# A two-layer encoder trunk on one core: output products of a feed-forward group issued behind the sixth product of the next group, and fewer accumulating transfers at a layer's middle

## The chip, the cores and the metric

The kernel runs on one core of a Trainium2 chip. The metric is the device time of one execution in microseconds; lower is better. Five engines of the core work side by side, each in the order of its own instruction stream: TensorE (PE in the profile; its weight loads are PEld), VectorE (DVE), ScalarE (ACT), GpSimd (POOL) and SyncE (SP). Sixteen DMA engines move data; in this kernel SP issues plain transfers and POOL the accumulating ones, which add what they read to what stands in on-chip memory.

## The reference

Two layers. Each normalises its input, projects it, mixes tokens by windowed pooling and by differential attention, adds the gated sum back, and then adds a gated feed-forward block:

```python
for i in range(DEPTH):                                  # 2 layers, x is 512 x 1024, float32
    proj = rmsnorm(x, norm1_g[i]) @ w_in[i]             # u_pool, q, k, v, g_a, g_b
    ...
    o = diff_attention(q, k, v, lam)
    attn_out = (rmsnorm(o, subln_g[i]) * (1.0 - lam_init)) ...
    pool_out = pool_mixer(u_pool, pool_w[i], pool_scale[i])
    merged = sigmoid(g_a) * pool_out + sigmoid(g_b) * attn_out
    x = x + merged @ w_out[i]
    gate, up = split(rmsnorm(x, norm2_g[i]) @ w_ffn_in[i], 2)   # hidden width 2816
    x = x + (silu(gate) * up) @ w_ffn_out[i]
return x
```

## The kernel before

**Number format.** Every product of two float32 matrices is three TensorE products: each operand is held as a high part (a rounded copy) and a low part (the difference), and high x high, high x low and low x high are summed (L280 to L282 and L299 to L301). A weight piece of 512 KB is loaded to a tile `raw` (L224, by SP, 7 buffers) and split into `whi` and `wlo` (6 buffers each). There are two ways to make the low part in `parts`: ACT copies the high part and DVE subtracts (L210, L211), or ACT writes the high part and the negated raw piece (L234, L235) and an accumulating transfer issued by POOL adds the raw piece from HBM once more (L236).

**A layer.** Four heads of attention and pooling run first; `last_out` then adds the second half of the `w_out` product to the residual `res`, 4 pieces of 2 products, and after each piece `Sets.put` makes operands of the new `res` for the feed-forward block. The feed-forward block has 22 hidden tiles of 128. The two odd ones (`odd_group`, tiles 20 and 21) are computed plainly. The other 20 are five groups of four (`GROUPS`), each made by seven products instead of eight, in the order `PRODUCTS = (1, 5, 6, 2, 7, 4, 3)`; each product is 24 TensorE matmuls of 512 columns. Weights of products 1, 2 and 4 are loaded and split with the accumulating transfer; those of 5, 6, 7 and 3 are sums and differences that DVE forms in the raw tiles (L860, L866, L867, L880).

**A hidden tile's way.** When products 2, 7, 4 and 3 of a group end, `Hidden.put` applies the gate (ACT tanh, two DVE operations), and after the second of two token blocks `turned` transposes blocks on DVE and sends the tile out to HBM and back in another order (L315 away, L317 four times near). `Hidden.back` then splits it into `fh` (ACT, L210) and `fl` (DVE, L211). It is put into the streams when the kernel's own count of TensorE columns has gone on by `HIDDEN_AWAY`, or when an output product needs it.

**Output products.** `out_unit` multiplies four hidden tiles (two for the odd group) by a piece of `w_ffn_out`: 12 matmuls into a bank `oy` or `mm`, and a DVE add into `res` (L685). `pair_units(f0, i)` loads one piece and makes two of them; a group has four such pairs. A pair of group g-1 stands behind each of products 6, 2, 7 and 4 of group g (`FILLED`); in group 0 the two halves of the odd group stand behind 6 and 2. The last group takes two pairs of its predecessor, the other two and its own four come at the end. `weight_plan` writes the pieces in the same order, so that the loads match.

**What sets the order.** TensorE's products and pairs are in program order, held by `in_turn` and `chained`. On DVE, ACT and SP a scheduler merges the streams by priority and by the free buffers, so an operation that waits holds all behind it on its engine.

**Start of layer 1.** The last pairs of layer 0 end in `next_x`, which also sums squares of the new `res` (L397, L401). `attention` multiplies four token blocks; after the first one (t = 0) `token_stats` sums the squares by small TensorE products (L412) in a bank `mm`.

Of the kernel before, what the change touches and what calls it, by code (L numbers as in the profile page):

```python
# [22 lines left out]
NT = S // P  # L23
# [16 lines left out]
GROUPS = (0, 4, 8, 12, 16)  # L40
PRODUCTS = (1, 5, 6, 2, 7, 4, 3)
LOADS = {1: ((0, 0),), 5: ((1, 0), (1, 4)), 2: ((0, 4),), 4: ((1, 4),)}
FILLED = (6, 2, 7, 4)
ODD = 20
# [8 lines left out]
QK_AWAY, SCORE_AWAY, PROB_AWAY, AV_AWAY, MERGE_AWAY = 28000, 26000, 32000, 18000, 24000  # L53
HIDDEN_AWAY = 22000


def weight_plan():
# [22 lines left out]
    for layer in range(L):  # L80
        for i, j in enumerate(ORDER):
            block("w_in", layer, qk(j))
            if i >= 2:
                for cb in range(2):
                    k = 2 * ORDER[i - 2]
                    block("w_out", layer, span((512 * cb, 512)), k, k + 2)
            block("w_in", layer, vg(j))
            if i:
                block("w_in", layer, ug(ORDER[i - 1]))
        block("w_in", layer, ug(ORDER[3]))  # L90
        ks = [2 * j + a for j in ORDER[2:] for a in range(2)]
        for d in range(4):
            plan.append(("w_out", layer, ks, span((P * d, P), (P * (d + 4), P))))

        for k in range(4):
            plan.append(("w_ffn_in", layer, (k, k + 4), gate_up(ODD)))

        def out(f0, pairs):
            for i in pairs:
                plan.append(("w_ffn_out", layer, range(f0, f0 + 4), span((256 * i, 256))))  # L100

        def quarter(f0, side, k0, h):
            plan.append(("w_ffn_in", layer, (k0 + 2 * h, k0 + 2 * h + 1), gate_up(f0 + 2 * side)))

        for g, f0 in enumerate(GROUPS):
            for n in PRODUCTS:
                for q in LOADS.get(n, ()):
                    for h in range(2):
                        quarter(f0, *q, h)
                if n in FILLED:  # L110
                    at = FILLED.index(n)
                    if not g:
                        if at < 2:
                            block("w_ffn_out", layer, span((512 * at, 512)), ODD, ODD + 2)
                    elif g < len(GROUPS) - 1 or at < 2:
                        out(GROUPS[g - 1], (at,))
        out(GROUPS[-2], (2, 3))
        out(GROUPS[-1], range(4))
# [4 lines left out]
def trunk_kernel(  # L123
# [81 lines left out]
    at = [0]  # L205
# [196 lines left out]

    def token_stats(full):

# [4 lines left out]
        squares[0] = None  # L409
        ss = mm_ps()[:, :NT]  # L410
        for t in range(NT):
# [60 lines left out]
    for layer in range(L):  # L472
# [14 lines left out]
        def attention(j, before, then):  # L487
# [88 lines left out]
            if not at_start:  # L576
                w = wblock(KD)
            for t in range(NT):
                if at_start:
                    acc = first_acc[t]  # L580
                    first_products(t, steps[2] + steps[3])
                    if not t:
                        token_stats(True)
                else:
                    acc = mm_ps()
                    product(acc, list(zip(x_tok(t), w)))
                    if layer and not t and j == ORDER[0]:
                        token_stats(True)
                qn = sb.tile([P, 4, QK], F32, name="qn", tag="qn", bufs=3)
# [9 lines left out]
                if not at_start:  # L599
                    qn = turned(qn.rearrange("p h c -> p (h c)"), 4, "qn", 3)  # L600
                later(17400 + 5700 * t if at_start else QK_AWAY, lambda t=t, qn=qn: turn(t, qn))
                if not t and then is not None:
                    then()
# [149 lines left out]
        def last_out(x):  # L753
            for i in range(4):
                w = piece(4, True)
                for a in range(2):
                    acc = mm_ps()
                    in_turn(acc, [(cols(w, a)[2 * n + h], (ms[j][0][:, h, :], ms[j][1][:, h, :]))
                                  for n, j in enumerate(ORDER[2:]) for h in range(2)])
                    add_out(i + 4 * a, acc)  # L760
                x.put(i)
# [35 lines left out]
        def odd_group(x):  # L797
            to = Hidden(ODD, *HIDDEN_AT[ODD])
            w = [piece(2, True) for _ in range(4)]
            accs = [mm_ps(), mm_ps(), tr_ps(), tr_ps()]  # L800
# [40 lines left out]
        def group(g, x):  # L841
# [8 lines left out]
            def prepare(n):  # L850
# [4 lines left out]
                elif n == 5:  # L855
                    raws[21], raws[1] = got
                    sets[5] = []
                    for h in range(2):
                        s1, r21 = raws[1][h][0], raws[21][h][0]
                        nc.vector.tensor_add(s1, r21, s1)  # L860
                        sets[5].append(parts(s1))
# [30 lines left out]
            for n in PRODUCTS:  # L892
# [36 lines left out]
                elif n == 3:  # L929
                    multiply(3, c, False)  # L930
                    for t in range(2):
                        nc.vector.tensor_add(x2[t], c[t], x2[t])
                        to[0].put(1, t, x2[t][:, :VD], x2[t][:, VD:])
                if n in FILLED:
                    at = FILLED.index(n)
                    if not g:
                        if at < 2:
                            odd_units(at)
                    elif g < len(GROUPS) - 1 or at < 2:
                        pair_units(GROUPS[g - 1], at)  # L940

# [31 lines left out]
        for g in range(len(GROUPS)):  # L973
            group(g, sets_of_x)
        for i in (2, 3):
            pair_units(GROUPS[-2], i)
# [59 lines left out]
```

## Time and profile before

| | us |
|---|---|
| median of 3 runs (lowest, highest) | 1509.73 (1505.37, 1521.37) |
| the profiled execution | 1509.37 |
| its span, first to last instruction | 1507.6 |
| DVE busy in the span | 1059.6 (70%) |
| ACT busy | 700.9 (46%) |
| POOL busy | 129.0 (9%) |

A row of the waits view reads: the engine, tile and line that waited, what ended the wait, then the sum of the waits in us, their number and the longest. A row of the windows view reads: the stretch in us from the span's start, its length, then for each engine the busy time and, in brackets, the number of instructions; then the mean TensorE clock granted in the stretch as a share of full speed, the mean busy share of the DMA engines and the GB/s moved. Durations of TensorE matmuls are modelled and overlap, so that a matmul of 389 ns is followed by the next one after less; what a matmul takes is read from a stretch without waits, as length by count.

### The profile page before, as it was taken

What the parts mean: (1) busy time and instruction counts of PE and PEld (TensorE: products, weight loads), DVE (VectorE), ACT (ScalarE), POOL (GpSimd) and SP (SyncE); (2) the same over time, 40 slices, a digit from 0 to 9 for tenths busy, and PEclk for the clock granted to TensorE, in tenths of its full rate; (3) what the DMA queues carried; (4) which work ended last, traced back from release to release, by engine and by line L of the source; (5) the groups of instructions that cost most, each with busy time, mean ns of one, the idle gap of its engine ahead of it and who ended that gap; (6) DMA issues with size and microseconds to landing.
All of it is one profiled execution on the core that took longest, in us unless ns stands there. A gap on an engine that the chain in (4) does not pass through costs nothing.

```text
span 1507.6 us, 18715 instructions
## 1 busy us (share of the span) xinstructions
PE 1414.3 (94%) x6242; PEld 1156.8 (77%) x6242; DVE 1059.6 (70%) x2055; ACT 700.9 (46%) x1310; POOL 129.0 (9%) x151
## 2 busy tenths in 40 slices
PE   9999999997888989898899999999998989898898
PEld 7888888886776867677678888888876767686686
DVE  7778687856756767575667797878576667585763
ACT  6453353455534444454344443535574443553540
POOL 1001000010100000000011101000110000000000
PEclk9999999998989999999999999999999999999999
DMA  8344444465666675757525454445566666757652
GB/s 291 100 141 138 145 138 131 146 155 139 150 171 194 171 205 149 218 158 211 160 65 159 121 178 159 126 133 158 147 154 167 175 187 169 216 149 222 159 162 84
DMA packets 145392, 241.30 MB, mean 160 GB/s; under 512 B 41360, under 2 KB 88976, under 8 KB 145296
## 3 DMA queue, kind: packets, MB, share of 16 engines
q1 hardware_dynamic: 133056, 198.14, 41.1%
q0 software_dynamic: 10944, 39.85, 14.4%
q10 hardware_dynamic: 1296, 2.12, 0.5%
q8 instruction: 49, 0.80, 0.2%
q14 instruction: 47, 0.39, 0.1%
HBM read 210.82 MB, written 29.23 MB: 159 GB/s over the span
## 4 chain that ended last, share of the span: by engine, by line
PE 64%; DMA 15%; DVE 11%; ACT 4%; issue 3%; SPq 2%; POOL 0%; ACTq 0%; DVEq 0%; POOLq 0%
PE mm L299 12%; PE mm L300 12%; PE mm L301 12%; DMA near<-away 8%; DMA away<-near 5%; DMA raw<-in_wts 3%; PE mm L280 3%; PE mm L281 3%; PE mm L282 3%; DVE wlo L211 2%; PE oy L280 2%; PE oy L281 2%; SPq L317 2%; PE oy L282 2%; PE sc L280 2%
## 5 line engine op out<-in xcount | busy, mean ns | idle before, releaser
L210 ACT CAST whi<-raw 128x1024 fp32r<-128x1024 f32 (+1 forms) x229 | 238.1, 1046 | 219.8 <-PE mm L281 87.5
L211 DVE TENSOR_TENSOR wlo<-raw,whi 128x1024 fp32r<-128x1024 f32 (+1 forms) x229 | 275.5, 1210 | 39.0 <-ACT whi L210 38.3
L299 PE MATMUL mm<-whi,xh 128*128 128x512 f32 x480 | 189.9, 396 | 0.0
L301 PE MATMUL mm<-whi,xl 128*128 128x512 f32 x480 | 188.2, 392 | 0.0
L300 PE MATMUL mm<-wlo,xh 128*128 128x512 f32 x480 | 188.1, 392 | 0.0
L280 PE MATMUL oy<-fh,whi 128*128 128x512 f32 (+1 forms) x180 | 80.2, 446 | 65.6 <-ACT fh L210 62.9
L236 POOL DMA_DIRECT2D wlo<-in_wts x76 | 66.6, 876 | 676.8 <-ACT wlo L235 631.4
L301 PEld LDWEIGHTS mm<-whi,xl 128*128 128x128 f32 x480 | 90.7, 189 | 19.4
L300 PEld LDWEIGHTS mm<-wlo,xh 128*128 128x128 f32 x480 | 90.9, 189 | 17.6
L299 PEld LDWEIGHTS mm<-whi,xh 128*128 128x128 f32 x480 | 90.9, 189 | 17.6
L685 DVE TENSOR_TENSOR res<-mm,res 128x512 f32<-128x512 f32 x96 | 65.0, 681 | 53.2 <-PE mm L282 49.0
L333 POOL TENSOR_TENSOR r<-r,mhalf 128x4 f32<-128x4 f32 (+1 forms) x64 | 58.0, 906 | 515.6 <-DVE r L332 442.6
L300 PE MATMUL mm<-xl,whi 128*128 128x512 f32 x256 | 99.8, 390 | 0.0
L299 PE MATMUL mm<-xh,whi 128*128 128x512 f32 x256 | 99.8, 390 | 0.0
L301 PE MATMUL mm<-xh,wlo 128*128 128x512 f32 x256 | 99.6, 389 | 0.0
L280 PEld LDWEIGHTS oy<-fh,whi 128*128 128x128 f32 x180 | 38.6, 215 | 79.4 <-ACT fh L210 68.0
L234 ACT CAST whi<-raw 128x1024 fp32r<-128x1024 f32 x76 | 79.3, 1043 | 37.5 <-PE mm L281 35.4
L280 PE MATMUL sc<-whi,xh 128*128 128x512 f32 x240 | 93.6, 390 | 0.0
L282 PE MATMUL sc<-whi,xl 128*128 128x512 f32 x240 | 93.4, 389 | 0.0
L281 PE MATMUL sc<-wlo,xh 128*128 128x512 f32 x240 | 93.4, 389 | 0.0
L235 ACT ACTIVATE wlo<-raw 128x1024 fp32r<-128x1024 f32 x76 | 80.4, 1057 | 25.1 <-PE sc L281 8.6
L281 PE MATMUL oy<-fl,whi 128*128 128x512 f32 (+1 forms) x180 | 79.4, 441 | 0.2 <-DVE fl L211 0.2
(241 smaller groups left out, 3188.9 us busy)
## 6 DMA issues: line engine op xcount, KB each, us to landing
raw<-in_wts SPq DMA_DIRECT2D x264, 512.0 KB, 4.5
wlo<-in_wts POOLq DMA_DIRECT2D x76, 512.0 KB, 8.1
away<-near SPq DMA_DIRECT2D x72, 256.0 KB, 2.2
near<-away SPq DMA_DIRECT2D x288, 64.0 KB, 2.7
away<-near SPq DMA_DIRECT2D x28, 128.0 KB, 1.7
near<-away SPq DMA_DIRECT2D x112, 32.0 KB, 2.4
res<-in_x_t SPq DMA_DIRECT2D x4, 512.0 KB, 7.0
pwr<-in_pool_w ACTq DMA_DIRECT2D x8, 256.0 KB, 2.7
```

The source lines that it names most:

```text
L210: ins = nc.scalar.copy(hi, src)
L211: nc.vector.tensor_sub(lo, src, hi.bitcast(F32))
L234: nc.scalar.copy(hi, raw)
L235: nc.scalar.activation(lo, raw, AF.Copy, scale=-1.0)
L236: nc.gpsimd.dma_start(lo.rearrange("p a b -> p (a b)"), wts[piece_no], accum_op=ALU.add)
L280: nc.tensor.matmul(acc, lhsT=ah, rhs=bh, start=start, stop=False, **check)
L281: nc.tensor.matmul(acc, lhsT=ah, rhs=bl, start=False, stop=False, **check)
L282: last = nc.tensor.matmul(acc, lhsT=al, rhs=bh, start=False, stop=stop, **check)
L299: nc.tensor.matmul(acc, lhsT=ah, rhs=bh, start=i == 0, stop=False)
L300: nc.tensor.matmul(acc, lhsT=ah, rhs=bl, start=False, stop=False)
L301: last = nc.tensor.matmul(acc, lhsT=al, rhs=bh, start=False, stop=i == n - 1)
L685: return nc.vector.tensor_add(res[d][:, cs], acc, res[d][:, cs])
```

## The change

Four edits.

1. `FILLED` goes, and `UNITS` says by (group, product) which output products stand behind it: the odd group's two halves behind products 7 and 4 of group 0; group 0's pairs behind 4 and 3 of group 1 and behind 1 and 5 of group 2; and so on, two pairs behind 4 and 3 of the next group and two behind 1 and 5 of the group after. All four pairs of group 3 come at the end, ahead of group 4's. `HIDDEN_AWAY` goes from 22000 to 42000 columns.
2. `last_out` makes the low parts of its four pieces on DVE, `odd_group` those of its pieces 0 and 2: 6 accumulating transfers and 6 ACT copies fewer in each layer, 6 DVE subtractions more.
3. In group 0 of a layer the adds that form product 5's weights (L860, now L871) are held behind the last add of `last_out` on DVE (`tc.issue_after(x.added.ins)`).
4. At the start of layer 1 the small products of `token_stats` come behind the second token block instead of the first, in a bank `sc` instead of `mm`; the first block's eviction is made after them.

```diff
-FILLED = (6, 2, 7, 4)
+UNITS = {(0, 7): [(-1, 0)], (0, 4): [(-1, 1)], (1, 4): [(0, 0)], (1, 3): [(0, 1)],
+         (2, 1): [(0, 2)], (2, 5): [(0, 3)], (2, 4): [(1, 0)], (2, 3): [(1, 1)],
...
+         (4, 1): [(2, 2)], (4, 5): [(2, 3)]}
...
-HIDDEN_AWAY = 22000
+HIDDEN_AWAY = 42000
...
-    def token_stats(full):
+    def token_stats(full, bank=mm_ps):
...
-        ss = mm_ps()[:, :NT]
+        ss = bank()[:, :NT]
...
+                    if layer and j == ORDER[0] and t < 2:
+                        held.append((t, acc))
+                        if not t:
+                            continue
+                        token_stats(True, s_ps)
+                        evicted(*held.pop(0))
+                evicted(t, acc)
...
         def last_out(x):
             for i in range(4):
-                w = piece(4, True)
+                w = piece(4)
...
-                    add_out(i + 4 * a, acc)
+                    x.added = add_out(i + 4 * a, acc)
...
-            w = [piece(2, True) for _ in range(4)]
+            w = [piece(2, k % 2 > 0) for k in range(4)]
...
-                        nc.vector.tensor_add(s1, r21, s1)
+                        with ExitStack() if g else tc.issue_after(x.added.ins):
+                            nc.vector.tensor_add(s1, r21, s1)
...
-                if n in FILLED:
-                    at = FILLED.index(n)
-                    if not g:
-                        if at < 2:
-                            odd_units(at)
-                    elif g < len(GROUPS) - 1 or at < 2:
-                        pair_units(GROUPS[g - 1], at)
+                for source, i in UNITS.get((g, n), ()):
+                    if source < 0:
+                        odd_units(i)
+                    else:
+                        pair_units(GROUPS[source], i)
...
-        for i in (2, 3):
+        for i in range(4):
             pair_units(GROUPS[-2], i)
```

Lines of the changed kernel are 1 to 11 higher than before's. The instruction order on TensorE at the end of product 6 in group 0 of layer 0 (`xrh`, `xrl` are product 6's operands, `fh`, `fl` hidden tiles, `sc` product 2's bank) was before:

```order
L280 MATMUL mm<-whi,xrh 128x512
L281 MATMUL mm<-wlo,xrh 128x512
L282 MATMUL mm<-whi,xrl 128x512
L280 MATMUL oy<-fh,whi 128x512
L281 MATMUL oy<-fl,whi 128x512
L282 MATMUL oy<-fh,wlo 128x512
```

and is in the changed kernel:

```order
L281 MATMUL mm<-whi,xrh 128x512
L282 MATMUL mm<-wlo,xrh 128x512
L283 MATMUL mm<-whi,xrl 128x512
L281 MATMUL sc<-whi,xh 128x512
L282 MATMUL sc<-wlo,xh 128x512
L283 MATMUL sc<-whi,xl 128x512
```

Product 2 follows product 6 at once, and the odd group's output products come behind product 7. On DVE in the middle of layer 0 (`res_85` to `res_88` are the residual's four tiles, `xg`, `xh`, `xl`, `xth`, `xtl`, `xrh`, `xrl` the operands that `Sets` makes) stood before:

```order
L685 TENSOR_TENSOR res_85<-mm,res_85 128x512
L211 TENSOR_TENSOR xl<-xg,xh 128x512
L211 TENSOR_TENSOR xtl<-xg,xth 128x256
L722 TENSOR_TENSOR xg<-xg 128x256
L724 TENSOR_TENSOR xg<-xg 128x256
L860 TENSOR_TENSOR raw<-raw 128x1024
L685 TENSOR_TENSOR res_87<-mm,res_87 128x512
L211 TENSOR_TENSOR xl<-xg,xh 128x512
L866 TENSOR_TENSOR raw<-raw 128x1024
```

and the same raw add stands in the changed kernel in this place, behind all adds into `res` of `last_out`:

```order
L734 TENSOR_TENSOR xg<-xg 128x256
L409 TENSOR_TENSOR sq_3890<-sq 128x512
L734 TENSOR_TENSOR xg<-xg 128x256
L212 TENSOR_TENSOR xrl<-xg,xrh 128x256
L871 TENSOR_TENSOR raw<-raw 128x1024 x2
L877 TENSOR_TENSOR raw<-raw 128x1024
L212 TENSOR_TENSOR wlo<-raw,whi 128x1024
```

The raw adds, which need two loaded pieces, moved from ahead of an add that frees a TensorE bank to behind the last such add.

More of the change, by code (lines that the diff above doesn't have):

```diff
@@ L109, in weight_plan @@
                         quarter(f0, *q, h)
-                if n in FILLED:
-                    at = FILLED.index(n)
-                    if not g:
-                        if at < 2:
-                            block("w_ffn_out", layer, span((512 * at, 512)), ODD, ODD + 2)
-                    elif g < len(GROUPS) - 1 or at < 2:
-                        out(GROUPS[g - 1], (at,))
-        out(GROUPS[-2], (2, 3))
+                for source, i in UNITS.get((g, n), ()):
+                    if source < 0:
+                        block("w_ffn_out", layer, span((512 * i, 512)), ODD, ODD + 2)
+                    else:
+                        out(GROUPS[source], (i,))
+        out(GROUPS[-2], range(4))
         out(GROUPS[-1], range(4))
@@ L577, in attention, with evicted @@
                 w = wblock(KD)
[L578 to L588, printed above, removed]
+            held = []
+            def evicted(t, acc):
                 qn = sb.tile([P, 4, QK], F32, name="qn", tag="qn", bufs=3)
@@ L601, in attention @@
                 later(17400 + 5700 * t if at_start else QK_AWAY, lambda t=t, qn=qn: turn(t, qn))
+            for t in range(NT):
+                if at_start:
+                    acc = first_acc[t]
+                    first_products(t, steps[2] + steps[3])
+                    if not t:
+                        token_stats(True)
+                else:
+                    acc = mm_ps()
+                    product(acc, list(zip(x_tok(t), w)))
+                    if layer and j == ORDER[0] and t < 2:
+                        held.append((t, acc))
+                        if not t:
+                            continue
+                        token_stats(True, s_ps)
+                        evicted(*held.pop(0))
+                evicted(t, acc)
                 if not t and then is not None:
@@ L933, in group @@
                         to[0].put(1, t, x2[t][:, :VD], x2[t][:, VD:])
[L934 to L937, printed above, removed]
-                            odd_units(at)
-                    elif g < len(GROUPS) - 1 or at < 2:
-                        pair_units(GROUPS[g - 1], at)
+                for source, i in UNITS.get((g, n), ()):
+                    if source < 0:
+                        odd_units(i)
+                    else:
+                        pair_units(GROUPS[source], i)
         def next_x(i):
```

1 row of the table UNITS is left out of this document.

## The prediction

> **What bounds the kernel now.** I read the page first, then the waits of PE, then windows over the stages that the waits point to.
>
> ```profile
> span 1507.6 us, 18715 instructions
> PE 1414.3 (94%) x6242; PEld 1156.8 (77%) x6242; DVE 1059.6 (70%) x2055; ACT 700.9 (46%) x1310; POOL 129.0 (9%) x151
> PEclk9999999998989999999999999999999999999999
> ```
>
> TensorE is busy for 94% of the span, so it is the bound, and two things remain to be won: its idle time, and the slices in which its granted clock is under full speed. The waits of PE say where it idles:
>
> ```profile
> PE oy L280 <- ACT fh L210: 62.9, 12, 7.6
> PE mm L280 <- DVE res L685: 12.1, 4, 8.5
> PE mm L412 <- DVE sq L408: 2.9, 1, 2.9
> PE oy L280 <- DVE res L685: 2.7, 2, 1.7
> PE tr L280 <- DVE cqn L932: 2.5, 5, 0.8
> PE mm L281 <- DVE ml L217: 1.3, 2, 0.7
> ```
>
> The first row is output products that wait for a hidden tile (`fh`); the second is mostly `last_out`; the third is the statistics at the start of layer 1. Windows over a stretch without a wait, over the two second halves of a layer (from `last_out` to the layer's end), and over the start of layer 1 price them:
>
> ```profile
> 484.90:528.42 43.52, 43.52 (x194) 1.00 0.64 166
> ...
> 337.17:759.24 422.07, 375.12 (x1570) 301.81 (x1568) 280.40 (x407) 196.09 (x261) 30.20 (x35) 0.94 0.64 175
> 759.24:775.08 15.84, 12.93 (x47) 10.47 (x46) 10.21 (x22) 5.79 (x16) 2.05 (x2) 0.78 0.12 34
> 1094.61:1504.34 409.73, 373.65 (x1581) 301.61 (x1579) 269.84 (x392) 185.04 (x246) 30.23 (x35) 0.95 0.62 168
> ```
>
> Without waits 192 matmuls (194 less two that overlap the edges) take 43.52 us, 0.2267 each. By the code, `last_out` has 96 matmuls, the odd group 96, the 35 products 840, the output products 528: 1560, or 353.7 us, and 0.8 for the statistics, 354.5. The half layers lose 422.1 - 354.5 = 67.6 and 409.7 - 354.5 = 55.3, the third stretch (38 full matmuls and 0.8) 15.8 - 9.4 = 6.4. In all 129.3 us are lost. Of these the first four wait rows are 80.6 and the small ones about 5. The remaining 43.7 is matmuls that run slowly: the clock is 0.94, 0.78 and 0.95 in these windows and 1.00 in the one without waits. So a wait of PE costs itself and some slow microseconds behind it.
>
> [...]
>
> **The change, part by part.**
>
> *Units moved, HIDDEN_AWAY 42000.* The wait is on the round trip of the last hidden tile:
>
> ```profile
> 590.91 0.39 PE L280 MATMUL sc<-whi,xh 128*128 128x512 f32 x1
> ...
> 613.83 0.79 PE L280 MATMUL oy<-fh,whi 128*128 128x512 f32 x1 [4.87 <-ACT fh L210]
> ```
>
> Product 3 ends at 590.9, the next group's products 1, 5, 6 take three times 24 x 0.2267 = 5.44, and the tile is ready at 613.8: a lag of 22.9 against 16.3 of cover (4.87 of it idle, the rest small waits and slow restarts). Behind product 4 the cover is six products, 32.6, or 43.5 with two pairs between. At the layer's end the four pairs of group 3 cover 21.8; there the lag was:
>
> ```profile
> 717.14 0.39 PE L280 MATMUL oy<-fh,whi 128*128 128x512 f32 x1
> ...
> 734.13 0.80 PE L280 MATMUL oy<-fh,whi 128*128 128x512 f32 x1 [4.00 <-ACT fh L210]
> ...
> 392.49 0.28 PE L412 MATMUL mm<-ones,sq 128*128 128x1 f32 x2
> ...
> 418.44 0.69 DVE L211 TENSOR_TENSOR fl<-near,fh 128x512 fp32r<-128x512 f32 x1 [3.89 <-ACT fh L210]
> ```
>
> 17.0, so 4.8 to spare. The odd group is tightest: from its statistics to `fl` 26.0, against 0.8 and five products, 28.0. It has 2 to spare. The returns `near` in the stretch 470 to 740 landed so after their issue:
>
> ```profile
> DMA to landing us min/median/max: 1.9/3.9/9.8
> ```
>
> So between nothing and 4 (the longest for the median, 5.9 more, less the 2) I book 1 per layer, near the lower end, since the lag measured already holds a slow return. The wait rows 62.9 and 2.7 go.
>
> HIDDEN_AWAY also moves `fl` on DVE. It held that engine:
>
> ```profile
> 584.27 0.48 DVE L784 SCALAR_TENSOR_TENSOR h<-th,stats,cta 128x256 f32<-128x256 f32 x1
> 590.14 0.69 DVE L211 TENSOR_TENSOR fl<-near,fh 128x512 fp32r<-128x512 f32 x1 [5.38 <-ACT fh L210]
> ```
>
> For 5.4 us everything behind `fl` stood, the next gate and the adds into `res` among them. 42000 columns are 42000 / 512 x 0.2267 = 18.6 us instead of 9.7, about the lag of one tile, so this hold nearly goes. PE did not wait on it, so I book no gain.
>
> What is late next are weights of products 2 and 4, which need an accumulating transfer, as the split buffers (6) are now handed on in another order. In the row of products 1, pair, 5, pair, 6, 2, 7, 4, pair, 3, pair the buffer of product 4's first half comes free in the middle of product 6; product 4 begins 2.72 + 5.44 + 5.44 = 13.6 us later (before, with pairs between, 19.0). To be done in it, by these rows of the page and of the stretch 470 to 740:
>
> ```profile
> L235 ACT ACTIVATE wlo<-raw 128x1024 fp32r<-128x1024 f32 x76 | 80.4, 1057 | 25.1 <-PE sc L281 8.6
> L234 ACT CAST whi<-raw 128x1024 fp32r<-128x1024 f32 x76 | 79.3, 1043 | 37.5 <-PE mm L281 35.4
> L236 POOL DMA_DIRECT2D wlo<-in_wts x76 | 66.6, 876 | 676.8 <-ACT wlo L235 631.4
> ...
> raw<-in_wts SPq DMA_DIRECT2D x58, 512.0 KB, 4.8
> wlo<-in_wts POOLq DMA_DIRECT2D x21, 512.0 KB, 8.3
> away<-near SPq DMA_DIRECT2D x16, 256.0 KB, 2.4
> near<-away SPq DMA_DIRECT2D x64, 64.0 KB, 3.9
> ...
> DMA to landing us min/median/max: 6.9/8.3/10.2
> ```
>
> 1.0 + 1.1 + 0.9 + 8.3 = 11.3, a margin of 2.3; with the longest landing, 10.2, 0.4. So the bound below is nothing; above, if landings stretch as the same traffic goes into 360 us instead of 422 (10.2 x 422 / 360 = 12.0), 1.4 us each on eight groups. I book 0.4 for each of ten, 4 in all.
>
> *Twelve accumulating transfers become DVE subtractions.* Removed: 12 x 1.06 on ACT, 12 x 0.88 on POOL and 6.3 MB of traffic; added: 12 x 1.21 = 14.5 on DVE:
>
> ```profile
> L211 DVE TENSOR_TENSOR wlo<-raw,whi 128x1024 fp32r<-128x1024 f32 (+1 forms) x229 | 275.5, 1210 | 39.0 <-ACT whi L210 38.3
> ...
> 339.28 16.02 DMA raw<-in_wts
> ...
> 355.42 1.23 DVE L860 TENSOR_TENSOR raw<-raw 128x1024 f32<-128x1024 f32 x1 [13.41 <-DMA raw<-in_wts]
> ...
> 357.90 0.79 PE L280 MATMUL mm<-mh,whi 128*128 128x512 f32 x1 [8.46 <-DVE res L685]
> ```
>
> The DVE work is hidden by the 13.4 us in which DVE stood there; in the half layer DVE goes from 280.4 of 422 to 287.7 of about 360, 80%. I book 0. Were that cover gone, six subtractions would cost 7 us per layer at most.
>
> *The raw add behind the last add into `res`.* The chain above is the whole wait: a load took 16.0, DVE waited 13.4 with the add for it ahead of the add into `res`, PE idled 8.5 (2.8 in layer 1). Behind the last `res` add it holds nothing that `last_out` needs, and product 5, which uses it, comes a full odd group and product 1 later, 96 x 0.2267 + 5.4 = 27 us. Gain 11.2 of the 12.1; the other 0.9 stays.
>
> *Statistics behind the second block.* The squares end 2.9 after block 0; block 1 adds 5.44 of cover. Gain 2.9. The first eviction comes 5.4 later; a fourth block needs its bank. From the statistics' products to its end it took 5.8, at the low clock:
>
> ```profile
> 767.75 0.38 PE L412 MATMUL mm<-ones,sq 128*128 128x1 f32 x2 [2.92 <-DVE sq L408]
> ...
> 772.67 0.86 DVE L596 SCALAR_TENSOR_TENSOR qn<-mm,r,hg 128x128 f32<-128x128 f32 x3
> ```
>
> Now block 2 and the statistics cover 5.44 + 0.8 = 6.2. Between 0 and 1 us, I book 0.
>
> *Clock.* Of the 43.7 slow microseconds about 7 stand behind the small waits that stay; 37 go with the long ones.
>
> Sum: 62.9 + 2.7 + 11.2 + 2.9 + 37 = 116.7 gained; 2 + 4 = 6 lost. The span 1507.6 - 116.7 + 6 = 1396.9; with the 1.8 around it (1509.4 - 1507.6) 1398.7. The profiled execution stands 0.4 under the median. I forecast 1399.
>
> **The rivals.**
>
> *Weights become late.* The accumulate margin of 2.3 goes negative as PE runs denser. For it speaks the DMA share, 0.64, which becomes 0.75; against it that ACT is at half load. At 2 to 5 us for eight groups, with 2.5 of slow clock each where the wait is over 2.9, the time is 1415 to 1459.
>
> *Waits stay.* The edit does not do what it says if the round trip stretches with its cover, since `away` and `near` stand in SP's stream among loads that wait for buffers. The 5.4 hold of DVE shows that a wait can move. If half of the 116.7 stays, 1457.
>
> *Slower.* In every group the raw adds (L871) still stand on DVE between product 4's two evictions, waiting for a load whose buffer comes free in product 7, one buffer earlier than the need. The 16.0 load in `last_out` speaks for it; against it the median landing of 4.8. DVE held for x us longer costs PE x - 8.2 (the next pair and half of product 3 need no bank of it) and 2.2 of clock; ten groups lose the whole gain at x = 17. At x = 20 the time is 1399 + 10 x 14 = 1539.
>
> *All lost time returns.* If the small waits vanish too, since DVE is no longer held by `fl`, and nothing new comes, the time is the bound, 1507.6 - 129.3 + 1.8 = 1380. Against it: the small waits are on tiles that the change doesn't touch (`cqn`, `ml`). [...]
>
> **How the numbers follow.** Forecast 0.66 (1388 to 1415), weights late 0.20, all returns 0.07, waits stay 0.04, slower 0.03. The range, 1384 to 1432, takes in the forecast and about the nearer half of the late weights and of what lies under it; 0.10 + 0.04 + 0.04 + 0.03, about 0.2, is left out. A measurement can tell about 1% here. Faster by over 1% is everything but the slower rival and a sliver of the others: 0.95; within 1% 0.03; slower 0.02.
>
> **What would show it.** Right: the row "oy <- fh" of PE's waits falls from 62.9 to under 5, the row "mm <- res" from 12.1 to about 1, the statistics' wait is gone, and the granted clock in the half layers is 0.99 or more. POOL has 64 transfers for 76. Wrong: a new PE wait on `wlo` at `sc` (products 2 and 4), which would be late weights; waits at the odd group's output products of over 3; or DVE idle before L871 in the groups. I would be wrong in the clock's term if the waits go and the slow matmuls stay.

## The result, and the profile after

The changed kernel takes 1410.68 us (median of 4 runs, 1408.86 to 1413.99), the kernel before 1512.12 in the runs made beside it. The ratio is 0.9328, with a 95% interval of 0.9273 to 0.9382: faster by 6.7%, 101 us. The forecast was 1399 with a range of 1384 to 1432. The profiled execution took 1410.3, with a span of 1408.5 where the forecast's sum had 1396.9, so 11.6 us more were lost than the sum had left.

The page of the changed kernel, its span, its engines and the granted clock:

```profile
span 1408.5 us, 18704 instructions
PE 1382.1 (98%) x6242; PEld 1140.7 (81%) x6242; DVE 1075.1 (76%) x2067; ACT 690.3 (49%) x1298; POOL 117.5 (8%) x139
PEclk9999999999999999999999999999999999999999
wlo<-in_wts POOLq DMA_DIRECT2D x64, 512.0 KB, 7.7
```

TensorE is busy for 98% of the span instead of 94, its granted clock is 9 tenths or more in every slice, DVE has the twelve subtractions more (2067 instructions for 2055), POOL the twelve transfers less (64). The waits of PE (total, times, longest):

```profile
PE oy L281 <- DVE res L695: 9.6, 4, 4.8
PE mm L300 <- DVE qn L589: 3.5, 2, 2.4
PE sc L282 <- DMA wlo<-in_wts: 2.2, 2, 1.1
```

The row "oy <- fh" (62.9) is gone, and so are the row "mm <- res" (12.1) and that of the statistics (2.9). What leads now is another row of the same products: `oy` no longer waits for its operand but for its bank, which an add into `res` on DVE must empty. The second row was one wait of 0.6 us before; its line is L596 in the kernel before and L589 in the changed one, since this block of code stands 7 lines higher there, not lower. Windows over the two halves that the change is about, the start of layer 1 between them, and over the two attention halves ahead of them (us, then the engines' busy time, at the end the granted clock, the DMA share and GB/s):

```profile
338.70:705.03 366.33, 359.61 (x1569) 295.25 (x1568) 282.16 (x408) 194.46 (x258) 28.76 (x33) 0.99 0.70 195
705.03:715.46 10.43, 10.43 (x48) 8.63 (x46) 6.77 (x7) 5.80 (x16) 0.00 (x0) 1.00 0.17 51
1037.90:1405.29 367.39, 359.83 (x1581) 295.69 (x1579) 271.21 (x393) 182.48 (x243) 28.67 (x33) 0.99 0.65 182
...
0.00:338.70 338.70, 335.19 (x1571) 277.43 (x1571) 263.09 (x641) 162.24 (x406) 30.25 (x41) 1.00 0.47 150
715.46:1037.90 322.44, 317.06 (x1480) 263.69 (x1478) 251.42 (x619) 145.34 (x376) 29.80 (x34) 1.00 0.46 141
```

Against the 354.5 us that their matmuls need, the half layers now lose 11.8 and 12.9 us (67.6 and 55.3 before), the start of layer 1 loses 10.4 - 9.4 = 1.0 (6.4 before). The attention halves, which the forecast left alone, grew: layer 0's from 337.17 to 338.70, layer 1's from 319.49 to 322.44, as the same two stretches of the kernel before show:

```profile
0.00:337.17 337.17, 335.56 (x1571) 278.07 (x1572) 257.35 (x636) 165.34 (x410) 34.11 (x45) 1.00 0.50 153
775.12:1094.61 319.49, 317.05 (x1479) 264.84 (x1478) 241.34 (x600) 148.64 (x380) 32.41 (x36) 1.00 0.48 145
```

That is 11.8 + 12.9 + 1.0 + 1.5 + 2.9 = 30.1 us lost where the sum had 129.3 - 116.7 + 6 = 18.6. (Layer 0's 1.5 is no effect of an edit: its first half has the same code in all kernels of this study, and lasted 337.0 to 339.0 in them.)

Most of the difference is one place in each layer, the output products of the odd group's second half (here the second odd unit). The timeline there, in layer 0, DMA queues, DVE and PE together (start, duration, engine, what, idle before it):

```profile
402.83 8.20 SPq L225 DMA_DIRECT2D raw<-in_wts  x5
411.32 0.33 SPq L316 DMA_DIRECT2D away<-near  x1
...
420.03 1.75 SPq L318 DMA_DIRECT2D near<-away  x4
...
423.99 0.69 DVE L212 TENSOR_TENSOR fl<-near,fh 128x512 fp32r<-128x512 f32 x1 [2.87 <-ACT fh L211]
424.60 2.35 DVE L871 TENSOR_TENSOR raw<-raw 128x1024 f32<-128x1024 f32 x2
...
428.07 1.21 DVE L877 TENSOR_TENSOR raw<-raw 128x1024 f32<-128x1024 f32 x1
...
430.67 0.68 DVE L695 TENSOR_TENSOR res<-oy,res 128x512 f32<-128x512 f32 x1
...
431.40 0.80 PE L281 MATMUL oy<-fh,whi 128*128 128x512 f32 x1 [3.98 <-DVE res L695]
```

Read it from below. PE waits 3.98 us at 431.4 for the add into `res` that empties its bank; DVE makes that add at 430.67, though the product to be added had ended at about 426; ahead of it stand the second group's raw adds, a gate and `fl`, the second part of the first group's first hidden tile. DVE idled 2.87 us for `fl`, because the tile came back late: its transfer `away` was issued at 411.32, and its return only at 420.03. The `away` transfers have a median of 2.9 us in this kernel; this one took

```profile
DMA to landing us min/median/max: 8.7/8.7/8.7
```

and the windows over the stretch suggest a reason (DMA share, the number before the last):

```profile
405.00:410.00 5.00, 5.00 (x23) 4.14 (x23) 2.60 (x6) 4.16 (x6) 0.88 (x1) 1.00 0.96 269
410.00:415.00 5.00, 5.00 (x23) 4.14 (x23) 4.74 (x7) 2.50 (x3) 0.00 (x0) 1.00 1.04 271
415.00:420.00 5.00, 4.63 (x20) 3.49 (x19) 4.92 (x11) 1.52 (x3) 0.00 (x0) 1.00 0.84 317
```

From 405 to 415 the DMA share is 0.96 to 1.04, with five loads of 512 KB and two accumulating transfers under way. Layer 1 shows the same picture, with a wait of 4.85. Behind the two waits matmuls run at half clock for 6.08 and 5.74 us, of which half, 3.0 and 2.9 us, is lost (an estimate).

### The profile page after: what moved, and what is told of

It is laid out like the page before. It is cut to its first block, busy times and chain, and to the rows that moved or that the text cites. A ratio compares the mean times of both kernels' runs of the same rounds, so it can differ in the third digit from the quotient of the medians.

```text
span 1408.5 us, 18704 instructions
## 1 busy us (share of the span) xinstructions
PE 1382.1 (98%) x6242; PEld 1140.7 (81%) x6242; DVE 1075.1 (76%) x2067; ACT 690.3 (49%) x1298; POOL 117.5 (8%) x139
## 4 chain that ended last, share of the span: by engine, by line
PE 76%; DVE 8%; DMA 6%; issue 5%; ACT 3%; POOL 2%; SPq 1%; DVEq 0%; POOLq 0%; ACTq 0%
PE mm L300 11%; PE mm L301 11%; PE mm L302 11%; PE mm L282 5%; PE mm L283 5%; PE mm L281 5%; DMA away<-near 3%; PE sc L282 3%; PE sc L283 3%; PE sc L281 3%; PE oy L281 3%; PE oy L283 3%; PE oy L282 3%; PE tr L281 2%; PE tr L282 2%
## 5 line engine op out<-in xcount | busy, mean ns | idle before, releaser
L211 ACT CAST whi<-raw 128x1024 fp32r<-128x1024 f32 (+1 forms) x241 | 250.8, 1047 | 217.9 <-PE mm L282 46.9
L212 DVE TENSOR_TENSOR wlo<-raw,whi 128x1024 fp32r<-128x1024 f32 (+1 forms) x241 | 292.0, 1214 | 61.2 <-ACT whi L211 59.7
L237 POOL DMA_DIRECT2D wlo<-in_wts x64 | 56.1, 876 | 569.8 <-ACT wlo L236 385.7
L334 POOL TENSOR_TENSOR r<-r,mhalf 128x1 f32<-128x1 f32 (+1 forms) x64 | 56.5, 884 | 525.3 <-DVE r L333 422.4
L281 PE MATMUL oy<-fh,whi 128*128 128x512 f32 (+1 forms) x180 | 71.1, 395 | 9.6 <-DVE res L695 9.6
L236 ACT ACTIVATE wlo<-raw 128x1024 fp32r<-128x1024 f32 x64 | 66.9, 1056 | 18.0 <-PE mm L282 14.0
L282 PE MATMUL oy<-fl,whi 128*128 128x512 f32 (+1 forms) x180 | 70.6, 392 | 0.0
L235 ACT CAST whi<-raw 128x1024 fp32r<-128x1024 f32 x64 | 66.5, 1039 | 8.3 <-PE mm L282 6.8
L283 PE MATMUL oy<-fh,wlo 128*128 128x512 f32 (+1 forms) x180 | 70.6, 392 | 0.0
```

The costliest lines, as they stand in the source:

```text
L211: ins = nc.scalar.copy(hi, src)
L212: nc.vector.tensor_sub(lo, src, hi.bitcast(F32))
L235: nc.scalar.copy(hi, raw)
L236: nc.scalar.activation(lo, raw, AF.Copy, scale=-1.0)
L281: nc.tensor.matmul(acc, lhsT=ah, rhs=bh, start=start, stop=False, **check)
L282: nc.tensor.matmul(acc, lhsT=ah, rhs=bl, start=False, stop=False, **check)
```

## The experiments

Times are medians of 4 runs (6 for the last kernel), each with runs of the kernel before on the same chip.

| Kernel | us | lowest to highest | ratio to before (95%) |
|---|---|---|---|
| changed | 1410.68 | 1408.86 to 1413.99 | 0.9328 (0.9273 to 0.9382) |
| units back | 1495.05 | 1491.39 to 1497.35 | 0.9884 (0.9849 to 0.9919) |
| HIDDEN_AWAY 22000 | 1411.49 | 1408.22 to 1412.24 | 0.9330 (0.9304 to 0.9355) |
| transfers back | 1409.35 | 1408.04 to 1410.91 | 0.9320 (0.9295 to 0.9345) |
| raw adds free | 1411.89 | 1411.01 to 1412.35 | 0.9336 (0.9312 to 0.9359) |
| both of these | 1425.87 | 1422.88 to 1426.80 | 0.9431 (0.9404 to 0.9457) |
| statistics back | 1410.52 | 1408.56 to 1411.62 | 0.9313 (0.9284 to 0.9342) |
| bank skipped | 1409.32 | 1407.38 to 1412.56 | 0.9328 (0.9305 to 0.9352) |
| first group by subtraction | 1404.40 | 1403.70 to 1405.05 | 0.9274 (0.9246 to 0.9302) |
| hidden part late | 1403.05 | 1401.98 to 1403.93 | 0.9265 (0.9237 to 0.9293) |
| raw adds late too | 1411.87 | 1411.09 to 1415.67 | 0.9332 (0.9296 to 0.9368) |
| put together | 1399.74 | 1397.03 to 1401.19 | 0.9261 (0.9238 to 0.9284) |
| put together, earlier due | 1398.06 | 1395.42 to 1398.97 | 0.9224 (0.9197 to 0.9250) |

The median of the kernel before lay between 1511.66 and 1515.02 in these sets of runs, so a difference of 2 or 3 us between two of the kernels decides nothing by itself; there the traces decide.

### What each edit is worth

**Units back.** The output units go back behind products 6, 2, 7, 4 of the next group; all else stays changed.

```diff
+UNITS = {(g, n): [(g - 1, i)] for g in range(4) for i, n in enumerate((6, 2, 7, 4)) if g or i < 2}
+UNITS.update({(4, 6): [(3, 0)], (4, 2): [(3, 1)]})
...
-        for i in range(4):
+        for i in (2, 3):
             pair_units(GROUPS[-2], i)
```

> The changed kernel with its output units where they were before (behind products 6, 2, 7, 4 of the next group, two pairs left over for the layer's end); everything else stays changed. Theory A, the cover in matmuls sets the waits: the row 'oy <- fh' returns with 45 to 65 us in 10 to 12 waits of 4 to 7 us, about 2.5 us of slow matmuls stand behind each, and the time is 1411 + 65 to 95, 1476 to 1506. Rival B, the later splitting of the hidden tiles (42000 columns) does the work and not the units' place: the row stays under 10 us and the time within 1400 to 1425.

The leading row of its waits of PE:

```profile
PE oy L279 <- ACT fh L209: 62.7, 12, 7.4
```

The row is back to 0.2 us, in as many waits as before, and the time rises by 1495.05 - 1410.68 = 84.4. Undoing the units' order gives back five sixths of the change, and theory A holds: the cover in matmuls decides, and the later splitting doesn't.

**HIDDEN_AWAY 22000.**

```diff
-HIDDEN_AWAY = 42000
+HIDDEN_AWAY = 22000
```

> The changed kernel with HIDDEN_AWAY at 22000 again. Theory A, the hold of DVE by the hidden tiles' second parts lies beside PE's work: PE's waits stay within 5 us of those of the changed kernel, the time is 1406 to 1420. Rival B, an early second part holds the engine that empties the banks: the waits on 'res' and on other DVE work grow by 1 to 5 us in most of the ten groups, time 1425 to 1460.

Measured 1411.49, 0.8 from the changed kernel and inside its runs. DVE's waits for a hidden tile, in the changed kernel and then in this one:

```profile
DVE fl L212 <- ACT fh L211: 22.3, 12, 3.7
```

```profile
DVE fl L212 <- ACT fh L211: 44.6, 14, 5.1
```

The later due time halves DVE's hold, and PE's time does not change by it. At the second odd unit the order on DVE is the same under both numbers, so the one hold that PE feels (waits of 3.84 and 5.11 here, 3.98 and 4.85 there) isn't moved by it.

**Transfers back, raw adds free, and both.** The first puts the twelve accumulating transfers back, the second takes away the order of the raw adds, the third does both.

```diff
-                w = piece(4)
+                w = piece(4, True)
...
-            w = [piece(2, k % 2 > 0) for k in range(4)]
+            w = [piece(2, True) for _ in range(4)]
```

```diff
-                        with ExitStack() if g else tc.issue_after(x.added.ins):
+                        with ExitStack():
                             nc.vector.tensor_add(s1, r21, s1)
```

> The changed kernel with the twelve accumulating transfers at the layers' middles restored (76 on POOL). Theory A, neither way is on the path: 1405 to 1417, no new wait on 'wlo' beyond 3 us in all. Rival B, the accumulating transfers are late at last_out and the odd group, with the traffic denser than before: new waits of 1 to 4 us at some of the twelve pieces, time 1420 to 1445. Under A the away transfer of the first group's first hidden tile (8.7 us in the changed kernel) stays at 6 to 10 us.

> The changed kernel without the order that puts the first group's raw adds behind the last add into res. Theory A, the add waited for a late load and held DVE: the waits of 8.5 and 2.8 us in last_out return with 2 us each of slow matmuls, time 1411 + 11 to 16, 1422 to 1427. Rival B, in the changed kernel these loads land earlier because six transfers fewer run in last_out: the wait is under 3 us in all, time 1409 to 1415.

The first came out by theory A (1409.35, waits on `wlo` 2.7 us in all, the `away` transfer at 8.4). The second didn't: 1411.89 and one wait of 1.5 us, rival B. Each edit undone by itself costs nothing that can be measured. So both were undone in one kernel:

> The changed kernel with both edits in last_out undone: the accumulating transfers are back and the raw adds are free to stand ahead of the adds into res. Undone one at a time they cost nothing (1409.4 and 1411.9). Theory A, either one alone removes the wait, because the load that the add waits for is late only when the split by transfer keeps the raw buffers in use longer, and a late load hurts only when the add stands ahead: the row 'mm <- res' returns with 8 to 14 us and 2 us of slow matmuls behind each wait, time 1420 to 1428. Rival B, neither removed it, but the units' new places changed the loads of last_out: no wait over 2 us, time 1407 to 1414.

It takes 15.2 us more than the changed kernel, by theory A. The wait in its waits of PE, and DVE's wait at the raw add, first with both undone, then with the raw adds free alone:

```profile
PE mm L281 <- DVE res L695: 11.9, 2, 8.8
```

```profile
356.44 1.23 DVE L871 TENSOR_TENSOR raw<-raw 128x1024 f32<-128x1024 f32 x1 [13.72 <-DMA raw<-in_wts]
```

```profile
344.41 1.23 DVE L871 TENSOR_TENSOR raw<-raw 128x1024 f32<-128x1024 f32 x1 [2.27 <-DMA raw<-in_wts]
```

With the transfers gone DVE has its load 12 us earlier, and an add that waits 2.3 us instead of 13.7 holds nobody for long, wherever it stands. With the add behind, a late load holds nobody either. The two edits are two cures for one wait.

Why the load is late is not as theory A has it. A raw buffer that comes free late, which it names, can delay only the issue: the load was issued at 339.98 with both undone and at 337.68 with the raw adds free alone, 2.3 us apart. From issue to landing it took, in the same order:

```profile
DMA to landing us min/median/max: 16.3/16.3/16.3
```

```profile
DMA to landing us min/median/max: 6.6/6.6/6.6
```

So about ten of the twelve microseconds are time in flight. With both undone POOL issued five accumulating transfers between 333.5 and 346.9, with the raw adds free alone one (338.0). The place of the adds has no part in it: with the transfers back and the adds late the same load took 16.1 us, in the changed kernel 8.1. So the split by transfer makes the load late, by its time in flight.

**Statistics back.** Behind block 0 again, in an `mm` bank.

```diff
-                    if layer and j == ORDER[0] and t < 2:
-                        held.append((t, acc))
-                        if not t:
-                            continue
-                        token_stats(True, s_ps)
-                        evicted(*held.pop(0))
+                    if layer and j == ORDER[0] and not t:
+                        token_stats(True)
```

> The changed kernel with the statistics at the start of layer 1 again straight behind block 0. Theory A: the wait of 2.9 us returns with 2 to 3 us of slow matmuls behind it, and the new waits of the attention half on qn (3.5 us in 2 waits) go, since the banks turn as before: 1410.7 + 5.5 - 3.5, 1409 to 1416. Rival B, the waits on qn have nothing to do with the move: they stay, and the time is 1414 to 1419.

Two rows of its waits of PE, and the window over layer 1's attention half:

```profile
PE mm L413 <- DVE sq L409: 2.9, 1, 2.9
...
PE mm L300 <- DVE qn L589: 0.6, 1, 0.6
```

```profile
716.96:1036.25 319.29, 316.99 (x1480) 264.86 (x1478) 247.92 (x608) 146.08 (x376) 28.67 (x32) 1.00 0.45 142
```

The statistics' wait returns, the waits on `qn` go, and the two cancel: 1410.52. The edit gained 3.9 us at the layer's start (14.3 there with it undone, 10.4 with it made) and gave back 3.2 in the attention half.

**Bank skipped.** Why it gives back was first put down to the banks.

```diff
+                if layer and j == ORDER[0] and t == NT - 1:
+                    mm_ps()
```

> The changed kernel with one accumulator bank skipped (allotted and not used) after the last block of layer 1's first attention step, so that from there the three banks turn as before the change, where the statistics took one of them. Theory A, the wait of 2.4 us at 846 (a merge product on a bank whose q and k are still being read, by qn) comes from the shifted turn: it goes, that of 1.0 at 739 stays or goes with it, layer 1's attention half falls from 322.4 to 319 to 321, time 1407 to 1409. Rival B, the wait comes from the statistics' later place: it stays within 0.3 us, time 1409 to 1413.

The waits of 1.03 and 2.43 stayed as they were: rival B. Theory A had overlooked that banks which turn round in a row keep their distances when all of them are shifted by one. The next theory, that the attention's pieces are issued a block too late, is in the last experiment.

### The wait at the second odd unit

**First group by subtraction.** The first group's products 1 and 2 are split on DVE: four accumulating transfers fewer in each layer, four DVE subtractions more.

```diff
-                    sets[1] = [parts(*r) for r in got[0]]
+                    sets[1] = [parts(r[0], r[1] if g else None) for r in got[0]]
...
-                    sets[2] = [parts(*r) for r in got[0]]
+                    sets[2] = [parts(r[0], r[1] if g else None) for r in got[0]]
```

> The changed kernel with the four accumulating transfers of the first group (products 1 and 2) made DVE subtractions, in both layers. Theory A, the away transfer of the group's first hidden tile lands late (8.7 us) because it stands behind weight traffic that fills the DMA engines, and two of these transfers are part of it: it lands in 3 to 6 us, DVE's hold by that tile (2.9 and 3.7 us) falls under 1.5 us, and PE's waits at the second odd unit (4.0 and 4.9 us) fall to 1 to 3. Time 1400 to 1408. Rival B, five raw loads alone fill the engines: the away transfer still takes over 6 us, the waits stay at 4 to 5, and DVE's four more subtractions (4.9 us per layer) make them longer by up to 2; 1410 to 1418.

The `away` transfer's landing, and the timeline of DVE:

```profile
DMA to landing us min/median/max: 5.8/5.8/5.8
```

```profile
422.05 0.68 DVE L212 TENSOR_TENSOR fl<-near,fh 128x512 fp32r<-128x512 f32 x1
...
427.82 0.68 DVE L695 TENSOR_TENSOR res<-oy,res 128x512 f32<-128x512 f32 x1
```

Theory A: the transfer lands in 5.8 for 8.7 us, `fl` finds its data there and waits for nothing, and the add into `res` comes 2.9 us earlier. PE's waits are 1.26 in both layers, no slow matmuls follow them, and the time is 1404.40. Less weight traffic makes the tile land earlier, but not in the way that the theory says. The two accumulating transfers that stand with the late tile belong to product 4, and both kernels issue them there (403.5 and 406.3; 403.3 and 406.1 here). The four that went had landed by 399.6, long before the tile was sent out at 411.3. The DMA share from 400 to 415 is no lower (1.05, 1.01 and 1.02 for 0.91, 0.96 and 1.04); what is ahead of the tile lands some 3 us sooner (product 4's second transfer at 414.9 for 418.1). Why 5.8 us remain, against a median of 2.9, stays open. A part comes back: the row "sc <- wlo" grew from 2.2 to 6.2 us.

**Hidden part late.** The traffic is left as it is; the second part of this one tile, which nobody needs before the second group's product 4, comes due later and is put behind an add of the odd units (in both layers of the trace the second of the second half's four).

```diff
-                    later(HIDDEN_AWAY, lambda: self.back(half, near))
+                    later(HIDDEN_AWAY if self.f0 or half else 50000, lambda: self.back(half, near))
...
+                    nc.scalar.copy(hi, near)
+                    with tc.issue_after(added[0].ins):
+                        nc.vector.tensor_sub(lo, near, hi.bitcast(F32))
```

> The changed kernel with the second part of the first group's first hidden tile on DVE put behind the last add of the odd units. Theory A, this instruction's wait holds the adds that empty the banks: PE's waits of 4.0 and 4.9 us at the second odd unit fall by 2 to 3.5 each, to 0.5 to 2.5, and with them the slow matmuls behind (3 us each); time 1398 to 1406. Rival B, the six microseconds of other DVE work behind it (raw adds, gates) set the wait: it falls by under 1 us each, the clock term stays, time 1408 to 1412. The away transfer itself stays at over 6 us under both.

1403.05, theory A: waits of 1.1 and 3.0 for 4.0 and 4.9, with `away` still at 7.9 us. So the late tile hurts by its place in DVE's order. What is left of the two waits is another hold: just ahead of these adds DVE now idles 1.25 and 3.12 us for `th`, ACT's tanh of a gate.

**Raw adds late too.**

```diff
-                        with ExitStack() if g else tc.issue_after(x.added.ins):
+                        with ExitStack() if g > 1 else tc.issue_after(added[0].ins if g else x.added.ins):
...
+                        with ExitStack() if g != 1 else tc.issue_after(added[0].ins):
+                            nc.vector.tensor_sub(r21, r11, r21)
```

> As the run before (the hidden tile's second part late), and the second group's three raw adds that stand ahead of these adds into res are put behind them too. Theory A, DVE's order alone makes the wait: the waits at the second odd unit go under 1 us and the clock term with them; what is late next is the second group's products 5 and 6, whose weights come from these adds, with 0 to 3 us per layer. Time 1395 to 1404. Rival B, the weights of the second group become late by as much as is won: waits on 'wlo' or 'whi' at products 5 and 6 of 3 to 6 us per layer, time 1406 to 1416.

Rival B in its size: 1411.87, 8.8 us worse than the run before. The waits at the odd unit did not fall further (1.4 and 2.8). Its first row of PE's waits:

```profile
PE sc L282 <- DMA wlo<-in_wts: 8.6, 5, 2.9
```

The place was forecast wrongly: not products 5 and 6 but product 2 of the second group and others that need accumulated weights are late.

### Put together

The tile's late part, the skipped bank, and subtractions for the first group's products 1 and 2 and the second group's product 2.

```diff
-                    sets[2] = [parts(*r) for r in got[0]]
+                    sets[2] = [parts(r[0], r[1] if g > 1 else None) for r in got[0]]
```

> Put together: the hidden tile's second part late, the skipped bank, and subtractions for the first group's products 1 and 2 and the second group's product 2. If the parts add (hold of DVE 6 to 8 us with 6 us of slow matmuls, late weights 2 us, attention 2.4 us): 1410.7 - 16 to 19, 1392 to 1396, with the row 'oy <- res' under 3 us and 'sc <- wlo' under 2. If a saved microsecond makes the weights of the groups behind late by the same (as in the runs with late waits on 'wlo' of 3.8 and 6.2): 1399 to 1405.

1399.74, 10.9 us under the changed kernel, with runs that don't overlap. Neither of the two forecasts had it quite: the row "sc <- wlo" is gone and the mean granted clock is 1.000, but the bank gives nothing, and a new wait came, of PE on DVE's gates:

```profile
PE sc L281 <- DVE h L799: 2.6, 2, 2.0
```

**Put together, earlier due.** The skipped bank is left out, and the first block's due time in layer 1 is drawn back by one block.

```diff
-                later(17400 + 5700 * t if at_start else QK_AWAY, lambda
+                later(17400 + 5700 * t if at_start else QK_AWAY - (12288 if layer and j == ORDER[0] and not t else 0), lambda
```

> The kernel best without the skipped bank, and with the due time of the first block's q and k in layer 1 (28000 columns) taken back by the 12288 columns of the one block by which the change puts it off. Theory A, the waits of 1.0 and 2.4 us on qn in layer 1's attention half come from its pieces being issued a block later: they go, that half falls from 322.9 to 318.5 to 320.5 us, and the time from 1399.7 to 1396 to 1398. Rival B, the pieces are now due before their data is there: the first block's transposes wait 1 to 5 us on qn's round trip, the half takes 321 to 326, the time is 1398 to 1403.

The window over layer 1's attention half, and the row on `qn`:

```profile
709.52:1029.68 320.16, 317.36 (x1480) 263.79 (x1478) 249.39 (x619) 144.97 (x376) 29.69 (x34) 1.00 0.46 141
```

```profile
PE mm L300 <- DVE qn L589: 0.3, 1, 0.3
```

Theory A: the half falls from 322.9 to 320.2, and the waits on `qn` go from 3.5 to 0.3 us. The statistics' move had put off the pieces of one block by 12288 columns, and with it the order of what follows. The total, 1398.06, is 1.7 lower; the runs of the two kernels overlap, since layer 1's second half lost 3.5 us again, in a wait on DVE's gate of 3.3 us and the slow matmuls behind it. Its median is the lowest of the kernels here, 0.9224 of the time before.

## Why the prediction was right, and where its steps were not

**The units (62.9, 2.7, and the clock behind them).** Right in mechanism and near in size: 65.6 us of waits and some 30 of the 37 of clock (an estimate: their share by the length of the waits), less 6 for what is late next, 90 in all, were forecast, 84.4 measured. No output product waits for a hidden tile any more.

**What is late next.** Two terms stood here. For the odd group's hidden tile 1 us per layer was booked: it came in time. For the weights of products 2 and 4 4 us: 2.2 measured, in two waits at the second group's product 2. Neither is what made the time 11.6 us longer than the sum.

**The step that failed** is the one on `fl`: "so this hold nearly goes. PE did not wait on it, so I book no gain". The hold went only to 22.3 us of 67.1, and in the first group it now stands ahead of adds that empty banks while PE has no slack. PE's waits there are 4.0 and 4.9 us, and 5.9 of slow matmuls follow them, 14.7 in all, more than the whole 11.6 by which the sum was short; layer 1's attention half adds 2.9, and the other terms together came out better than booked. Not all of the 14.7 is the tile: with its part put late the time fell by 7.6 us, and waits of 1.1 and 3.0 stayed, behind a gate. Behind the failed step stands a second error. The lag of a tile was stretched only by its return `near`; its outward transfer was taken at its usual time, and that was the one to be late, 8.7 us for 2.9. The sign that the prediction had named as wrong, waits over 3 at the odd group's output products, is what the trace shows. The run with the tile's part late shows the first link, its place on DVE; the run with less traffic shows that an earlier tile shortens the waits, and leaves open what in the traffic makes it late.

**last_out.** Forecast 11.2 and its part of the clock (3.4 by the trace before) for the raw adds' place, nothing for the transfers; undoing both measured 15.2. The sum was right, the division was not: either edit alone takes the wait away. The transfers were priced only by what they free on ACT, POOL and in bytes, and not by the landing of the loads issued among them (16.3 us with them, 6.6 without).

**Statistics.** 2.9 and its part of the clock (3.4 by the trace before) forecast, 0 in the total. The wait went as forecast; 3.2 us of it came back in the attention half, by the shifted due time. The step left out was that an eviction moved in the code moves all that is timed from it.

**Clock.** This term was too large. The prediction took as clock all lost time that is no wait, 43.7 us, and booked 37 of it. In the trace before the clock is at half for 99.0 us, and TensorE is busy for 65.2 of them. Matmuls of 512 columns stand 0.43 us apart there, 0.23 at full clock, so slow matmuls cost about half of the 65.2, 32.6: 25.7 behind the waits for hidden tiles, 3.4 in `last_out`, 3.4 behind the statistics. In the changed kernel it is 13.7 us at half clock, 11.8 of them busy, 5.9 lost. So 26.7 came back where 37 were booked: 4.4 had never been there, and 5.9 are new, at the second odd unit. The other 33.8 of the 99.0 us lie inside waits and are counted with them. The other 11 us of the 43.7 are not half clock; no view here splits them. The step that was right is that the slow matmuls go with the waits: the mean granted clock went from 0.967 to 0.995.

**Luck.** Against the sum, 14.7 at the odd unit, 4.4 of clock and 4.4 in the attention halves were lost, and 3.8 of the 6 booked for late work were not. That makes 19.7 us, and 11.6 were measured: some 8 us were won for which the prediction had no term.

Undone one at a time (the two edits of `last_out` together), the steps are worth 84.4 for the units, 15.2 for `last_out`, 0.8 for HIDDEN_AWAY and 0 for the statistics, 100.4 of the 101.4 measured.

**The rivals.** Late weights took 2.2 us, not 16 to 60; with PE denser still they grew (3.8, 6.2, 8.6 in the runs above), so the mechanism was there, and small. The slower rival had the right engine and the right instruction in the queue (L871 ahead of an add that empties a bank) but the wrong wait: DVE's wait for L871's load is 6.2 us over the whole kernel; it was `fl` that waited.

## What to carry to other kernels

- When the waits of the bound engine go, a hold of a second engine that had cost nothing comes into reach. Price such a hold against the slack after the change, not before: what stands behind it in that engine's order, and which of it empties a bank.
- A round trip through memory has two legs, and either can be late: here it was the outward one, 8.7 us for a median of 2.9, at a DMA share of 0.96 to 1.04. If a tile isn't needed soon, its consumer is cheap to put behind work that is; that was worth 7.6 us here, and delaying work that feeds a long weight path lost 8.8.
- Undo edits in pairs as well as alone. Two edits that each "cost nothing" when undone were worth 15 us together.

## What the hardware showed

The length of a wait did not decide alone here whether the clock halved. In the kernel before (start-up aside) no half clock follows PE's waits of 1.04, 1.66 and 2.03 us, and it follows all fourteen from 2.76 to 8.46 (the prediction's rival of late weights counted it only over 2.9). In the changed kernel it follows those of 3.98 and 4.85 us, and none of 1.03, 1.12, 1.12 and 2.42. The same wait, 2.42 or 2.43 us at the same merge product of layer 1, was met in eleven kernels. In five of them (transfers back, raw adds free, both of these, bank skipped, HIDDEN_AWAY 22000) eight or nine of the matmuls behind it stand 0.43 us apart; in five (changed, first group by subtraction, hidden part late, raw adds late too, put together) they stand 0.23 apart.

The clock's own record shows more. In the traces of the kernel before and of the changed one there are 16 stretches at half clock (but for the run's end). Within each trace they begin whole multiples of 3.413 us apart, and they last 3.41, 6.83 or 10.24 us (1, 13 and 2 times), one, two or three windows of that length. Here are such windows around the same wait of 2.43 us, first in the kernel with the raw adds free, then in the kernel put together (stretch, length, PE's busy time with its matmuls, clock, DMA share, GB/s):

```profile
843.37:846.78 3.41, 0.98 (x5) 1.00 0.93 318
846.78:850.20 3.42, 3.42 (x9) 0.50 0.17 49
850.20:853.61 3.41, 3.41 (x16) 1.00 0.51 147
```

```profile
839.15:842.56 3.41, 1.94 (x9) 1.00 0.91 280
842.56:845.97 3.41, 2.45 (x11) 1.00 0.44 139
```

In the first the wait lies inside one window, PE is busy for 0.98 of it, and the next window runs at half clock: 9 matmuls in it, and 16 in the full one after it. In the second the same wait is spread over two windows, in which PE idles 1.47 and 0.96 us, and the clock stays at 1.00. Cut at the same spacing, the traces of the kernel before and of the changed one have 820 windows at full clock. In the 16 that half clock follows PE idled 1.97 us or more, in the other 804 at most 1.77. The wait of 2.9 us at the statistics lay inside one of the 16, which was idle for 2.91 us.

What a wait cost in clock did not grow in step with its length. In the kernel before, the wait of 8.46 us has 10.24 us at half clock, over half of that inside it, and PE is busy for 3.87 of them, with 9 matmuls. The wait of 4.00 us has 6.83 us, 6.51 of them busy, with 15 matmuls; that of 2.92 has 6.83, busy throughout. Half of the busy time is what each cost in clock, 1.9, 3.3 and 3.4 us (an estimate). So a wait of 3 us cost more in clock here than one of 8, and cutting a wait from 4.0 to 1.3, as in the first group by subtraction, gained twice.
